# Decay products of a chunked scan: contraction over all 128 rows with a masked left tile

## The chip, the cores and the metric

One core of a Trainium2 chip. The metric is device time in microseconds (us) for one execution of the whole kernel. TensorE (PE) multiplies, VectorE (DVE), ScalarE (ACT) and GpSimd (POOL) do the elementwise work, and SyncE (SP) issues the DMAs; each engine takes its own instructions in order and waits on semaphores for the others.

## What is computed

One step of a hybrid decoder layer over 1,024 prompt tokens and 32 sample tokens: a spatial-gating MLP, a Mamba-2 scan and a memory attention read the same normalised input, and one output projection joins them. The change lies in the scan. It works in chunks of 128 tokens, and inside a chunk each of 8 heads needs a 128 x 128 matrix of decays:

```
acum   = jnp.cumsum(dt * a, axis=2)                       # running sums of the chunk
diff   = acum[:, :, :, None] - acum[:, :, None, :]
decay  = jnp.exp(jnp.where(causal, diff, -jnp.inf))
y_diag = jnp.einsum('bclgn,bcsgn,bclsgk,bcsgkp->...', cm, bm, decay, x * dt)
```

## The kernel before, in words

Nearly all of the time goes to projections. Every float32 operand is split into a part H and a remainder L, and a projection is a triple of matmuls for each of 8 row blocks (`gemm3`, L290 H x H, L291 L x H or H x L, L292 the third), here of 128 x 128 by 352 columns. Other work runs beside them: after each row block `hook()` adds a pace to a counter, and each time it passes 1 it runs the next step of a generator. So the order of the instructions on every engine is fixed when the program is built: a step's instructions stand between two triples on PE.

While the q, gg and part of the mg projections run, that generator is `scan()` (L825 on). It has 16 chunks, 2 groups of heads by 8 chunks of tokens, and in the loop over chunk i it prepares chunk i + 1:

- `sC(i)`: the chunk's C is split into CH (ACT, L107) and CL (DVE, L110).
- `sA(i + 1)`, L755 to L775: four transposes and a C B product on PE, then on DVE `xdt` (L772), `cbm` (L773) and `BL` (L110), on POOL `xsD` (L775).
- one step later `sE(i + 1, 0)`, and one step after that `sE(i + 1, 1)`: the decay products of four heads each, L808. `sE(i, 0)` is followed on ACT by Relu and Exp (L813, L815), `sE(i, 1)` by a min on DVE (L812) and an Exp on ACT (L816). `sM` (L820) multiplies the result `MT` by `cbm` on DVE.
- then the products with the state and into it (`mm3`, L797 to L799, contraction over 128 rows, 512 columns), `hT` times the chunk's decay on POOL (L877), 16 small products L882, and the elementwise tail (L888, L889, L903, L718, L906, L732 on DVE).

A decay product makes diff for four heads by 512 columns at once: the left tile holds 8 + 8 rows of negated running sums (H and L) and two rows of ones, the right tile the ones that pick a head and the running sums as rows. That is 18 rows for a chunk. The tiles `Lt` and `Rt` (128 rows) hold four chunks, chunk i on the 18 rows from q = 32 (i % 4) on, and the product takes these rows of both. The raw rows arrive in `Lraw` and `Rraw` by DMA: `chunk_rows` (L611 to L619) issues 16 DMAs for four chunks on SP (L617, L618), and `lr_copy`, once in four chunks, casts both to float32r on DVE (L750, L751) and calls `chunk_rows` for the next four.

The stream of weights runs beside that: at the end of some gemms (`w_tick`) a unit of 128 x 1024 is split, `wh` on ACT (L107), `wl` on DVE (L110), and SP's DMA of a later unit (L169) waits for that `wl`.

Of the kernel before, what the change touches and what calls it, by code (L numbers as in the profile page):

```python
# [58 lines left out]
def hybrid_step(ctx, tc, x_prompt, x_sample, mem_prompt, state_ssm, state_conv, cache_mem_k,  # L59
# [25 lines left out]
    # every float32 operand of the large products is split exactly into a float32r part (H) and  # L85
    # a float32r remainder (L); products are H*H + H*L + L*H, accumulated in float32
# [17 lines left out]
    def split(raw, H, L, heng, leng):  # L104
        """H = float32r(raw), L = raw - H"""
        if heng is ACT:
            ACT.activation(out=H, in_=raw, func=AF.Copy)  # L107
        else:
            heng.tensor_copy(out=H, in_=raw)
        leng.tensor_tensor(out=L, in0=raw, in1=rb(H), op=ALU.subtract)  # L110

# [114 lines left out]
    # 1 where the token belongs to the batch: 0 <= p - 4 b <= 3  # L226
# [17 lines left out]
    class RowNorm:  # L244
        """rows xt [T, 1024] -> dH + dL [128, 8, T] = (rmsnorm(xt) * g)^T"""

        bufs = 2
# [25 lines left out]
    # work that runs beside the large products: stepped between their parts  # L273
# [12 lines left out]
    def gemm3(ps, lhs, rhs, k0, kn, first, last, mid=None):  # L286
        """ps += sum over k of lhs(k)^T rhs(k) in three float32r products"""
        for k in range(k0, k0 + kn):
            (lH, lL), (rH, rL) = lhs(k), rhs(k)
            PE.matmul(out=ps, lhsT=lH, rhs=rH, start=(first and k == k0), stop=False)  # L290
            PE.matmul(out=ps, lhsT=lH, rhs=rL, start=False, stop=False)  # L291
            PE.matmul(out=ps, lhsT=lL, rhs=rH, start=False, stop=(last and k == k0 + kn - 1))  # L292
            if mid is not None and k == 3:
                mid()
            hook()
# [10 lines left out]
    def gemmA(w, mH, mL, t0, n):  # L306
        """weights stationary: [128 channels, n tokens]"""
        ps = mm()
        gemm3(ps[:, :n], lambda k: (w[0][:, k, :], w[1][:, k, :]),
              lambda k: (mH[:, k, t0:t0 + n], mL[:, k, t0:t0 + n]), 0, KD, True, True)  # L310
        w_tick()
        return ps

    def gemmS(wp, n, dst):
        """the 32 sample tokens stationary, H and L side by side: [dst = 32 tokens, n channels]; the weights
        are released"""
        ps = mm()
        for k in range(KD):
            wH, wL = wp[k // 4][0][:, k % 4, :], wp[k // 4][1][:, k % 4, :]
            if k > 0:  # L320
                PE.matmul(out=ps[:32, :n], lhsT=xS[:, k, 0:32], rhs=wL, start=False, stop=False)
            PE.matmul(out=ps[:64, :n], lhsT=xS[:, k, :], rhs=wH, start=(k == 0), stop=(k == KD - 1))
            if k == 0:
                PE.matmul(out=ps[:32, :n], lhsT=xS[:, k, 0:32], rhs=wL, start=False, stop=False)
            if k == 3:
                w_half()
            hook()
        w_done(1)
        ACT.activation(out=dst, in_=ps[:32, :n], func=AF.Copy)
        DVE.tensor_tensor(out=dst, in0=dst, in1=ps[32:64, :n], op=ALU.add)  # L330
        w_tick()

    def gemmB(mH, mL, t0, T, wp, n, last=False):
        """tokens stationary: [T tokens, n channels]; after the last tile the weights are released"""
        ps = mm()
        gemm3(ps[:T, :n], lambda k: (mH[:, k, t0:t0 + T], mL[:, k, t0:t0 + T]),
              lambda k: (wp[k // 4][0][:, k % 4, :], wp[k // 4][1][:, k % 4, :]), 0, KD, True, True,
              w_half if last else None)
        if last:
            w_done(1)  # L340
        w_tick()
        return ps

    # =====================================================================
    # Phase B: Mamba-2
    # =====================================================================
# [22 lines left out]
    Lt = bp.tile([128, 128], F32R, name="Lt")  # L369

# [24 lines left out]
    # the activation table is loaded while the first rows arrive  # L395
# [15 lines left out]
    def setup_side():  # L411
# [5 lines left out]
        # conv state, transposed  # L417
# [7 lines left out]
        # rows of the decay products: rows 0-7 and 8-15 pick a head (1 on its columns), 16-17 hold  # L425
        # the running sums (H, L) of the chunk
        POOL.memset(Lraw, 1.0)
        POOL.memset(Rraw, 1.0)
        POOL.affine_select(out=Rraw[0:8], in_=Rraw[0:8], pattern=[[1, 8], [0, 128]], compare_op=ALU.is_equal,
# [49 lines left out]
    # parameter vectors, one 128-vector per row, then transposed  # L479
# [22 lines left out]
    def x_side(t):  # L502
        # beside the products of tile t: transposes of tile t + 1, norm of tile t + 2
        if t + 5 < NTILE:
            x_load(t + 5)
        if t + 1 < NTILE:
            rn[t + 1].s2(0)
            yield
            rn.pop(t + 1).s2(1)
            if t + 1 == NTILE - 1:  # L510
                ACT.activation(out=xS[:, :, 0:32], in_=rb(xH[:, :, NP:NT]), func=AF.Copy)
                DVE.tensor_copy(out=xS[:, :, 32:64], in_=rb(xL[:, :, NP:NT]))
            yield
        if t + 3 < NTILE:
            x_s1a(t + 3)
            rn[t + 3].s1b()
# [18 lines left out]
    def dt_chain(pool):  # L535
# [10 lines left out]
        # log1p(e) = ln(u) * e / (u - 1), or e where u == 1  # L546
# [9 lines left out]
        # dta = -exp(a_log) * dt  # L556
# [46 lines left out]
        chunk_rows(0)  # L603
        for _ in range(4):
            yield
        DVE.tensor_copy(out=Lt, in_=Lraw)
        DVE.tensor_copy(out=Rt, in_=Rraw)
        chunk_rows(4)

    def chunk_rows(i0):  # L610
        """rows of chunk i % 8 of group i // 8, four of them"""  # L611
        for i in range(i0, i0 + 4):
# [3 lines left out]
            for e in range(2):  # L616
                SP.dma_start(out=Lraw[q + 8 * e:q + 8 * e + 8, :], in_=neg_d[e, r0:r0 + 8, :])  # L617
# [98 lines left out]
    def gate_norm(pool, y, sz, T):  # L716
        """y = y * sz; returns the scale to unit mean square; y, sz [T, 512]; sz is overwritten"""
# [29 lines left out]
    def lr_copy(i):  # L747
        """decay rows of chunks i .. i + 3"""
        if i < 16:
            DVE.tensor_copy(out=Lt, in_=Lraw)  # L750
            DVE.tensor_copy(out=Rt, in_=Rraw)  # L751
            if i + 4 < 16:
                chunk_rows(i + 4)

    def sA(i):  # L755
# [8 lines left out]
        s_.cbm = cp.tile([128, 128], F32, tag="cbm", name="cbm", bufs=1)  # L764
        ps = sd()
# [22 lines left out]
    def sC(i):  # L788
        """the chunk's C, for the product with the state"""
# [11 lines left out]
    def sE(i, j):  # L801
        """masked decays of four heads (transposed): exp(min(diff, 0))"""
        q = 32 * (i % 4)
        s_ = S[i]
        if j == 0:
            s_.MT = cp.tile([128, 8, 128], F32, tag="MT", name="MT", bufs=2)
        ps = sd()
        PE.matmul(out=ps, lhsT=Lt[q:q + 18, :],  # L808
                  rhs=Rt[q:q + 18, 4 * j:4 * j + 4, :].rearrange("p h l -> p (h l)"), start=True, stop=True)
# [19 lines left out]
    def scan():  # L829
# [14 lines left out]
        for i in range(16):  # L844
# [35 lines left out]
            for h in range(8):  # L880
# [3 lines left out]
                if h == 3:  # L884
                    if (i + 2) % 4 == 0:
                        lr_copy(i + 2)
# [53 lines left out]
    def sample_scan(sp2):  # L940
# [39 lines left out]
        # H, L, H of B against H, H, L of x: one pass over 96 rows  # L980
# [111 lines left out]
    def softmax_rows(pool, ps, n):  # L1092
        """ps [128, n, 256] scores -> P [128, n, 256]"""
# [133 lines left out]
    # =====================================================================  # L1227
    # Phase A: spatial-gating MLP
    # =====================================================================
# [90 lines left out]
    def mix(h):  # L1320
        """mixes head h; the result takes the place of v: vt[:, c, h] = [channels, tokens of chunk c]"""
# [52 lines left out]
    TB = [(0, 384), (384, 384), (768, 288)]  # L1374

    def outproj(H, L, first, at=None):
        units = [(ct, b) for ct in range(8) for b in range(3)]
        if first:
            # the last tokens are split last
            units[2:5] = units[3:5] + units[2:3]  # L1380
# [34 lines left out]
    def splitA(c, leng=DVE):  # L1415
        """all heads of token tile c"""
# [53 lines left out]
    # =====================================================================  # L1470
    # Phase C: memory cross-attention
    # =====================================================================
# [168 lines left out]
    def y_load(i):  # L1641
        """summed output of the other branches: the block's tokens of one channel tile"""
# [23 lines left out]
    # the output weights stay: the first ones in the slots of the stream  # L1666
# [20 lines left out]
    def rows_part(b, ct):  # L1687
        """transposes of one channel tile back to token rows, plus the residual"""
# [15 lines left out]
        if ct in SQE:  # L1704
# [12 lines left out]
            # the gain, once the squares are taken  # L1717
# [91 lines left out]
```

## Time and profile before

| | us |
|---|---|
| median of 3 runs | 1352.23 (1350.95 to 1352.24) |
| span of the profiled execution | 1351.7 |
| PE busy | 1320.8 (98%) |
| DVE busy | 590.4 (44%) |
| ACT busy | 496.5 (37%) |
| POOL busy | 210.4 (16%) |

For the profiled execution only its span is given, no separate device time; the median lies 0.5 us above the span. In rows of a timeline the first two numbers are the start in us from the start of the span and the duration in us, then engine, line, operation, output tile <- input tiles, shapes, and the count; square brackets give the idle time before it and what ended it. Matmuls overlap in these rows, so what one costs is read from the start of one to the start of the next. In a row of a group, "xN | busy, mean" is the count, the busy us and the mean ns of one. PEclk is the granted TensorE clock as a share of 2.4 GHz. The scan's decay products stand between 269 and 462 us of the span.

### The profile page before, as it was taken

What the parts mean: (1) busy time and instruction counts of PE and PEld (TensorE: products, weight loads), DVE (VectorE), ACT (ScalarE), POOL (GpSimd) and SP (SyncE); (2) the same over time, 40 slices, a digit from 0 to 9 for tenths busy, and PEclk for the clock granted to TensorE, in tenths of its full rate; (3) what the DMA queues carried; (4) which work ended last, traced back from release to release, by engine and by line L of the source; (5) the groups of instructions that cost most, each with busy time, mean ns of one, the idle gap of its engine ahead of it and who ended that gap; (6) DMA issues with size and microseconds to landing.
All of it is one profiled execution on the core that took longest, in us unless ns stands there. A gap on an engine that the chain in (4) does not pass through costs nothing. (4 is left out here: it accounts for less than half of the span.)

```text
span 1351.7 us, 22582 instructions
## 1 busy us (share of the span) xinstructions
PE 1320.8 (98%) x9231; PEld 1236.4 (91%) x9231; DVE 590.4 (44%) x943; ACT 496.5 (37%) x962; POOL 210.4 (16%) x274
## 2 busy tenths in 40 slices
PE   8999999999999999999999999999999889999996
PEld 7999999988888898888779999998999889999996
DVE  6212545566767632422112245345312646654543
ACT  6323444464545432222211124344313633322322
POOL 4200000043434424200000010002000600000122
PEclk9999999999999999999999999999999999999999
DMA  6223111122222245475551114221423565436432
GB/s 223 78 77 99 44 48 48 47 88 76 78 72 88 82 118 165 149 226 179 181 181 45 32 32 127 68 68 44 144 93 128 177 178 182 151 117 193 139 121 95
DMA packets 171595, 151.44 MB, mean 112 GB/s; under 512 B 13781, under 2 KB 155049, under 8 KB 171493
## 3 DMA queue, kind: packets, MB, share of 16 engines
q1 hardware_dynamic: 171492, 150.01, 36.1%
q8 instruction: 72, 1.18, 0.4%
q14 instruction: 31, 0.25, 0.1%
HBM read 111.97 MB, written 37.79 MB: 111 GB/s over the span
## 5 line engine op out<-in xcount | busy, mean ns | idle before, releaser
L290 PE MATMUL ps_mm<-xH,wh 128*128 128x352 f32 x1056 | 359.9, 341 | 0.0
L292 PE MATMUL ps_mm<-xH,wl 128*128 128x352 f32 x1056 | 339.6, 322 | 0.0
L291 PE MATMUL ps_mm<-xL,wh 128*128 128x352 f32 x1056 | 339.2, 321 | 0.0
L290 PEld LDWEIGHTS ps_mm<-xH,wh 128*128 128x128 f32 x1056 | 198.3, 188 | 25.3 <-issue 21.0
L291 PEld LDWEIGHTS ps_mm<-xL,wh 128*128 128x128 f32 x1056 | 199.0, 188 | 0.7
L292 PEld LDWEIGHTS ps_mm<-xH,wl 128*128 128x128 f32 x1056 | 198.4, 188 | 0.0
L110 DVE TENSOR_TENSOR wl<-wr,wh 128x1024 fp32r<-128x1024 f32 (+2 forms) x106 | 121.8, 1161 | 175.2 <-ACT wh L107 174.8
L290 PE MATMUL ps_mm<-wh,xH 128*128 128x256 f32 (+1 forms) x512 | 148.0, 289 | 0.0
L291 PE MATMUL ps_mm<-wl,xH 128*128 128x256 f32 (+1 forms) x512 | 146.4, 286 | 0.1
L292 PE MATMUL ps_mm<-wh,xL 128*128 128x256 f32 (+1 forms) x512 | 145.6, 284 | 0.3 <-DVE xL L110 0.3
L107 ACT ACTIVATE wh<-wr 128x1024 fp32r<-128x1024 f32 (+3 forms) x113 | 101.7, 915 | 36.2 <-PE ps_mm L291 14.2
L292 PEld LDWEIGHTS ps_mm<-wh,xL 128*128 128x128 f32 x512 | 98.1, 192 | 0.6 <-DVE xL L110 0.5
L290 PEld LDWEIGHTS ps_mm<-wh,xH 128*128 128x128 f32 x512 | 97.8, 191 | 0.4
L291 PEld LDWEIGHTS ps_mm<-wl,xH 128*128 128x128 f32 x512 | 97.7, 191 | 0.4 <-POOL wl L110 0.4
L701 ACT ACTIVATE gt<-ps_mm 128x352 f32<-128x352 f32 x72 | 33.0, 458 | 98.2 <-PE ps_mm L292 77.1
L290 PE MATMUL ps_mm<-aH,wh 128*128 128x384 f32 (+1 forms) x192 | 62.7, 327 | 1.9 <-ACT gt L1403 1.0
L290 PE MATMUL ps_mm<-bH,wh 128*128 128x384 f32 (+1 forms) x192 | 64.0, 334 | 0.0
L291 PE MATMUL ps_mm<-aL,wh 128*128 128x384 f32 (+1 forms) x192 | 63.0, 328 | 0.3
L292 PE MATMUL ps_mm<-bH,wl 128*128 128x384 f32 (+1 forms) x192 | 62.4, 325 | 0.2 <-DVE wl L110 0.2
L291 PE MATMUL ps_mm<-bL,wh 128*128 128x384 f32 (+1 forms) x192 | 62.5, 326 | 0.0
L292 PE MATMUL ps_mm<-aH,wl 128*128 128x384 f32 (+1 forms) x192 | 61.9, 323 | 0.0
L1720 POOL TENSOR_TENSOR xres<-xres,gfin 128x1536 f32<-128x1536 f32 (+3 forms) x6 | 14.4, 2392 | 231.6 <-ACT junk L1714 231.6
(385 smaller groups left out, 2472.8 us busy)
## 6 DMA issues: line engine op xcount, KB each, us to landing
wr<-in_w_in_dram SPq DMA_DIRECT2D x60, 512.0 KB
wr<-in_w_out_dram SPq DMA_DIRECT2D x24, 512.0 KB
kv<-in_cache_mem_k_dram SPq DMA_DIRECT2D x16, 512.0 KB
kv<-in_cache_mem_v_dram SPq DMA_DIRECT2D x16, 512.0 KB
y_d<-gt SPq DMA_DIRECT2D x32, 192.0 KB
q_d<-gt SPq DMA_DIRECT2D x24, 176.0 KB
gg_d<-gt SPq DMA_DIRECT2D x24, 176.0 KB
mg_d<-gt SPq DMA_DIRECT2D x24, 176.0 KB
```

What stands on the lines that cost most here:

```text
L107: ACT.activation(out=H, in_=raw, func=AF.Copy)
L110: leng.tensor_tensor(out=L, in0=raw, in1=rb(H), op=ALU.subtract)
L290: PE.matmul(out=ps, lhsT=lH, rhs=rH, start=(first and k == k0), stop=False)
L291: PE.matmul(out=ps, lhsT=lH, rhs=rL, start=False, stop=False)
L292: PE.matmul(out=ps, lhsT=lL, rhs=rH, start=False, stop=(last and k == k0 + kn - 1))
L701: ACT.activation(out=t[:, :BLK], in_=ps[:, :BLK], func=func)
L1720: eng.tensor_tensor(out=t[:, 0:nf, c0:c0 + w], in0=t[:, 0:nf, c0:c0 + w], in1=gc.unsqueeze(1).to_broadcast([128, nf, w]), op=ALU.mult)
```

## The change

`Lt` is no longer a tile for four chunks. A mask `qmask` [128, 4] holds 1 on rows 32q to 32q + 17 of column q, 0 elsewhere. `sA(i)` begins with a new instruction on DVE, which multiplies all of `Lraw` by the mask's column of the chunk and writes a float32r tile `Lt` of the chunk's own; right behind it the two DMAs for the L rows of chunk i + 4 are issued. The product takes all 128 rows of `Lt` and of `Rt`. The R rows keep their cast and their DMAs once in four chunks.

```diff
+        POOL.memset(qmask, 0.0)
+        for q in range(4):
+            POOL.memset(qmask[32 * q:32 * q + 18, q:q + 1], 1.0)
...
-        chunk_rows(0)
+        r_rows(0)
+        for i in range(4):
+            l_rows(i)
...
-        DVE.tensor_copy(out=Lt, in_=Lraw)
         DVE.tensor_copy(out=Rt, in_=Rraw)
-        chunk_rows(4)
+        r_rows(4)
...
+    def l_rows(i):
+        if i < 16:
+            g, c = divmod(i, 8)
+            q = 32 * (i % 4)
+            r0 = c * 16 + g * 8
+            for e in range(2):
+                SP.dma_start(out=Lraw[q + 8 * e:q + 8 * e + 8, :], in_=neg_d[e, r0:r0 + 8, :])
...
-    def lr_copy(i):
+    def r_copy(i):
         if i < 16:
-            DVE.tensor_copy(out=Lt, in_=Lraw)
             DVE.tensor_copy(out=Rt, in_=Rraw)
             if i + 4 < 16:
-                chunk_rows(i + 4)
+                r_rows(i + 4)
...
     def sA(i):
...
+        s_.Lt = cp.tile([128, 128], F32R, tag="Lt", name="Lt", bufs=1)
+        DVE.tensor_scalar(out=s_.Lt, in0=Lraw, scalar1=qmask[:, i % 4:i % 4 + 1], scalar2=None, op0=ALU.mult)
+        l_rows(i + 4)
         ps = sd()
...
     def sE(i, j):
-        q = 32 * (i % 4)
         s_ = S[i]
...
-        PE.matmul(out=ps, lhsT=Lt[q:q + 18, :],
-                  rhs=Rt[q:q + 18, 4 * j:4 * j + 4, :].rearrange("p h l -> p (h l)"), start=True, stop=True)
+        PE.matmul(out=ps, lhsT=s_.Lt, rhs=Rt[:, 4 * j:4 * j + 4, :].rearrange("p h l -> p (h l)"), start=True, stop=True)
```

On DVE, in the stretch where the scan passes from chunk 7 to chunk 8 (a unit of weights is split there, and C of chunk 7), before:

```order
L718 TENSOR_TENSOR xsD<-xsD,sz 128x512
L906 TENSOR_TENSOR hL<-hT,hH 128x512
L732 TENSOR_TENSOR xsT<-ps_sd,vecs 128x4x128
L110 TENSOR_TENSOR wl<-wr,wh 128x1024
L110 TENSOR_TENSOR CL<-bcT,CH 128x128
L772 TENSOR_TENSOR xdt<-ps_sd,dt_all 128x512
L773 TENSOR_TENSOR cbm<-ps_sd,triu 128x128
L110 TENSOR_TENSOR BL<-ps_sd,BH 128x128
```

The same place after the change:

```order
L730 TENSOR_TENSOR xsD<-xsD,sz 128x512
L919 TENSOR_TENSOR hL<-hT,hH 128x512
L744 TENSOR_TENSOR xsT<-ps_sd,vecs 128x4x128
L110 TENSOR_TENSOR wl<-wr,wh 128x1024
L110 TENSOR_TENSOR CL<-bcT,CH 128x128
L778 TENSOR_SCALAR Lt<-Lraw,qmask 128x128
L787 TENSOR_TENSOR xdt<-ps_sd,dt_all 128x512
L788 TENSOR_TENSOR cbm<-ps_sd,triu 128x128
L110 TENSOR_TENSOR BL<-ps_sd,BH 128x128
```

The new instruction that makes the chunk's `Lt` stands behind the split of C (and of the weights, where there is one) and ahead of `xdt`.

On PE, around the first decay product of a chunk, with the semaphores that the product waits for, before:

```order
L292 MATMUL ps_mm<-xH,wl 128x352
L808 MATMUL ps_sd<-Rt,Lt 128x512 [waits DVE_49]
L290 MATMUL ps_mm<-xH,wh 128x352
L291 MATMUL ps_mm<-xL,wh 128x352
L292 MATMUL ps_mm<-xH,wl 128x352
```

The same place after the change:

```order
L292 MATMUL ps_mm<-xH,wl 128x352
L822 MATMUL ps_sd<-Rt,Lt 128x512 [waits DVE_49,PE_49]
L290 MATMUL ps_mm<-xH,wh 128x352
L291 MATMUL ps_mm<-xL,wh 128x352
L292 MATMUL ps_mm<-xH,wl 128x352
```

No instruction moved on PE. The product waited for DVE before as well, for the last DVE instruction that read its PSUM bank; now the instruction waited for is the one that makes `Lt`, one step ahead. PE_49 is PE's own count.

## Rows read from the trace of the kernel before

**Rows 1.** The page: busy time of PE over the whole span, and the granted TensorE clock in 40 slices of it, in tenths (9 is 90% or more).

```profile
PE 1320.8 (98%) x9231; PEld 1236.4 (91%) x9231; DVE 590.4 (44%) x943; ACT 496.5 (37%) x962; POOL 210.4 (16%) x274
...
PEclk9999999999999999999999999999999999999999
```

**Rows 2.** Timeline of PE around one decay product, 300.2 to 301.5 us.

```profile
300.38 0.32 PE L292 MATMUL ps_mm<-xH,wl 128*128 128x352 f32 x1
300.63 0.50 PE L808 MATMUL ps_sd<-Rt,Lt 18*128 18x512 f32 x1
301.06 0.43 PE L290 MATMUL ps_mm<-xH,wh 128*128 128x352 f32 x1
301.33 0.32 PE L291 MATMUL ps_mm<-xL,wh 128*128 128x352 f32 x1
```

**Rows 3.** The line L808 by itself: count, least, median and greatest duration in ns, first and last start in us.

```profile
L808 PE MATMUL ps_sd<-Rt,Lt x32: 489/496/500, 269.1 to 461.3; 18*128 18x512 f32 x32
```

**Rows 4.** Timeline of PE where products over 128 rows with 512 columns pass back into the triples, 304.6 to 305.4 us.

```profile
304.64 0.39 PE L798 MATMUL ps_sd<-xdL,BH 128*128 128x512 f32 x1
304.87 0.39 PE L799 MATMUL ps_sd<-xdH,BL 128*128 128x512 f32 x1
305.10 0.32 PE L290 MATMUL ps_mm<-xH,wh 128*128 128x352 f32 x1
305.26 0.32 PE L291 MATMUL ps_mm<-xL,wh 128*128 128x352 f32 x1
```

**Rows 5.** Groups of instructions on DVE: the cast of `Lt` that goes, and two of the same kind as the new instruction, with a source in SBUF (L1744) and in PSUM (L812).

```profile
L750 DVE CAST Lt<-Lraw 128x128 fp32r<-128x128 f32 x3 | 0.7, 218 | 0.0
...
L1744 DVE TENSOR_SCALAR xres<-xres,rs 128x512 f32<-128x512 f32 x8 | 3.5, 482 | 1.4 <-POOL rs L1732 1.4
...
L812 DVE TENSOR_SCALAR MT<-ps_sd 128x512 f32<-128x512 f32 x16 | 11.0, 687 | 9.2 <-PE ps_sd L808 9.2
```

**Rows 6.** Timeline of PE: the projection's matmul right ahead of the first decay product of chunks 0, 1, 7, 8, 13 and 14.

```profile
268.82 0.32 PE L292 MATMUL ps_mm<-xH,wl 128*128 128x352 f32 x1
...
274.21 0.32 PE L292 MATMUL ps_mm<-xH,wl 128*128 128x352 f32 x1
...
353.57 0.32 PE L292 MATMUL ps_mm<-xH,wl 128*128 128x352 f32 x1
...
366.72 0.32 PE L292 MATMUL ps_mm<-xH,wl 128*128 128x352 f32 x1
...
433.17 0.32 PE L292 MATMUL ps_mm<-xH,wl 128*128 128x352 f32 x1
...
446.34 0.32 PE L292 MATMUL ps_mm<-xH,wl 128*128 128x352 f32 x1
```

**Rows 7.** Timeline of DVE: what stands right ahead of the place of the new instruction at chunks 0, 1, 3, 7, 8 (two rows), 13 and 14.

```profile
268.64 0.83 DVE L662 SCALAR_TENSOR_TENSOR bcT<-raw,vecs,bcT 128x32 f32<-128x32 f32 x3
...
276.13 1.29 DVE L820 TENSOR_TENSOR MT<-MT,cbm 128x512 f32<-128x512 f32 x2 [0.96 <-ACT MT L816]
...
298.92 0.29 DVE L110 TENSOR_TENSOR CL<-bcT,CH 128x128 fp32r<-128x128 f32 x1 [0.31 <-ACT CH L107]
...
352.45 1.21 DVE L110 TENSOR_TENSOR CL<-bcT,CH 128x128 fp32r<-128x128 f32 x1 [0.65 <-ACT CH L107]
...
365.99 1.74 DVE L110 TENSOR_TENSOR wl<-wr,wh 128x1024 fp32r<-128x1024 f32 x1 [0.92 <-ACT wh L107]
367.65 1.13 DVE L110 TENSOR_TENSOR CL<-bcT,CH 128x128 fp32r<-128x128 f32 x1
...
432.03 1.22 DVE L110 TENSOR_TENSOR CL<-bcT,CH 128x128 fp32r<-128x128 f32 x1 [0.66 <-ACT CH L107]
...
447.29 1.13 DVE L110 TENSOR_TENSOR CL<-bcT,CH 128x128 fp32r<-128x128 f32 x1
```

**Rows 8.** Timeline of POOL: what runs there when DVE comes to the place of the new instruction, at chunks 1, 7, 8, 13 and 14.

```profile
277.21 1.35 POOL L110 TENSOR_TENSOR xdL<-xde,xdH 128x512 fp32r<-128x512 f32 x1 [3.95 <-ACT xdH L107]
...
353.46 1.10 POOL L775 TENSOR_TENSOR xsD<-xsD,dsk_b 128x512 f32<-128x512 f32 x1
...
368.60 1.09 POOL L877 TENSOR_TENSOR hT<-hT,dec 128x512 f32<-128x512 f32 x1
...
433.06 1.09 POOL L775 TENSOR_TENSOR xsD<-xsD,dsk_b 128x512 f32<-128x512 f32 x1
...
448.23 1.09 POOL L877 TENSOR_TENSOR hT<-hT,dec 128x512 f32<-128x512 f32 x1
```

**Rows 9.** Waits of PE over the whole span: line waited at, releaser, us in total, times, longest.

```profile
PE ps_sd L1561 <- DVE qL L110: 3.5, 1, 3.5
...
PE ps_mm L292 <- DVE woL L110: 2.1, 1, 2.1
```

**Rows 10.** Busy time by stretch: window, its length, then busy us (instructions) of PE, PEld, DVE, ACT and POOL, the granted TensorE clock, DMA share and GB/s. The first two follow the 3.5 us wait of the rows before, the third the 2.1 us wait.

```profile
1106.00:1108.00 2.00, 2.00 (x11) 2.00 (x10) 0.02 (x1) 1.89 (x4) 0.00 (x0) 0.52 0.92 286
1108.00:1110.00 2.00, 2.00 (x9) 2.00 (x8) 1.43 (x5) 1.05 (x3) 0.00 (x0) 0.63 0.30 100
...
1270.00:1272.00 2.00, 2.00 (x7) 1.92 (x8) 2.00 (x4) 0.00 (x0) 0.00 (x0) 0.50 0.00 0
```

**Rows 11.** Waits of SP between 268 and 480 us: its DMA of a weight unit, us in total, times, longest.

```profile
SPq L169 <- DVE wl L110: 68.2, 10, 9.7
```

**Rows 12.** Weight loads of PE (PEld) in the scan's stretch, 268 to 476 us.

```profile
L291 PEld LDWEIGHTS ps_mm<-xL,wh 128*128 128x128 f32 x257 | 48.6, 189 | 0.7
```

More of the change, by code (lines that the diff above doesn't have):

```diff
@@ L368, in hybrid_step @@
     Rt = bp.tile([128, 8, 128], F32R, name="Rt")
-    Lt = bp.tile([128, 128], F32R, name="Lt")
+    qmask = bp.tile([128, 4], F32, name="qmask")
     sc_ctx = ExitStack()
@@ L602, in dt_chain, with r_rows @@
         yield
-        chunk_rows(0)
+        r_rows(0)
+        for i in range(4):
+            l_rows(i)
         for _ in range(4):
             yield
-        DVE.tensor_copy(out=Lt, in_=Lraw)
         DVE.tensor_copy(out=Rt, in_=Rraw)
-        chunk_rows(4)
-    def chunk_rows(i0):
+        r_rows(4)
[6 more added lines that the diff above has]
+                SP.dma_start(out=Lraw[q + 8 * e:q + 8 * e + 8, :], in_=neg_d[e, r0:r0 + 8, :])
+    def r_rows(i0):
         for i in range(i0, i0 + 4):
@@ L616, in chunk_rows @@
             for e in range(2):
-                SP.dma_start(out=Lraw[q + 8 * e:q + 8 * e + 8, :], in_=neg_d[e, r0:r0 + 8, :])
                 SP.dma_start(out=Rraw[q + 16 + e:q + 17 + e].rearrange("p h l -> p (h l)"),
@@ L885, in scan @@
                     if (i + 2) % 4 == 0:
-                        lr_copy(i + 2)
+                        r_copy(i + 2)
                     if c > 0:
```

## The prediction

> **What bounds the kernel now.** I read the page first: PE is busy 98% of a span of 1351.7 us, at a granted clock of 9 tenths or more in all 40 slices [rows 1]. So time is won or lost only on PE, as matmul time or as new idle time, and DVE (44%), ACT and POOL matter only where PE waits for them. Next came the timeline of PE around one decay product, read from start to start. The L292 ahead of it begins at 300.38, the product at 300.63, the L290 behind it at 301.06 and the next L291 at 301.33 [rows 2]. So 0.95 us pass from that L292 to that L291. All 32 products look like this (489 to 500 ns each) [rows 3]. Then I read the same timeline where products over 128 rows with the same 512 columns run: they follow each other every 0.23 us, and the first triple member behind them is also back after 0.23; members of a triple follow each other every 0.16 [rows 4]. Last I read DVE and POOL at the place where the new instruction will stand.
>
> **The gain: the product itself.** With 128 rows the product should sit in the stream like those of L798 and L799. From L292 to L291 that makes 0.16 (L292 to the product), 0.23 (the product) and 0.16 (L290 to L291), together 0.55 in place of 0.95 [rows 2, 4]. A product gains 0.40 us and 32 of them **12.8 us**. The columns stay 512, so the gain is not in the arithmetic but in the empty time on both sides: 0.25 in place of 0.16 ahead, 0.43 in place of 0.23 under the product, and 0.27 in place of 0.16 behind the L290. The Trainium skill names the cause that fits (TensorEngine Tiling (Array Packing), section Tiling Modes, Key Properties): a change of tiling mode, here to 32 rows and back, drains TensorE; no number stands there, and the traces so far agree as far as 0.40 us a product goes.
>
> **The price: a wait for DVE.** Before, both operands lay ready for chunks. Now `sE(i, 0)` needs `Lt(i)`, which DVE makes one step ahead of it, and DVE takes its work in order, so whatever stands before `Lt(i)` there comes first. For each chunk I compare when PE wants to start, which is the start of the L292 ahead plus 0.16, with when `Lt` could be done: the end of what DVE does before it, plus the new instruction. That instruction is not in the trace; the nearest row is the cast of the same tile that it replaces, 0.22 [rows 5], and I take 0.2.
>
> - Chunk 0: wanted at 268.82 + 0.16 = 268.98; DVE is in the convolution until 268.64 + 0.83 = 269.47; ready at 269.67, late by 0.7 [rows 6, 7].
> - Chunk 1: wanted at 274.37; DVE multiplies both halves of `MT` of chunk 0 until 277.42; ready at 277.62, late by 3.25 [rows 6, 7]. Before, nothing on PE needed that in this step.
> - Chunks 7, 10, 12 and 13 (first and last shown): the split CL ends at 353.66 and 433.25, `Lt` is ready at 353.86 and 433.45, wanted at 353.73 and 433.33; late by 0.1 each [rows 6, 7].
> - Chunks 8, 11 and 14 (first and last shown): a unit of weights is split ahead of CL (365.99 for 1.74), so CL ends at 368.78 and 448.42; `Lt` at 368.98 and 448.62, wanted at 366.88 and 446.50; late by 2.1 each [rows 6, 7].
> - Chunks 2 to 6, 9 and 15: in time. At chunk 3 CL ends at 299.21 and the product was wanted at 300.54 [rows 2, 7].
>
> The lateness adds up to 0.7 + 3.25 + 4 x 0.1 + 3 x 2.1 = 10.7 us. In each of these 9 chunks the weight load (`Lt` is the stationary side) can't run ahead under other matmuls; it takes 0.19 [rows 12], so up to 9 x 0.19 = 1.7 more: **12.4 us**, about the whole gain.
>
> **Does the new instruction wait for POOL?** CL alone took 0.29 (chunk 3) and 1.13 to 1.22 where POOL was at work [rows 7, 8]: an operation on DVE with two sources in SBUF doesn't go on while POOL has its turn. The new one has one source (and a column of scalars). No row shows such an operation beside POOL, so I bound it: 0.2, or 0.2 after the end of the POOL operation under way. POOL does run at just these places [rows 8]: to 278.56 at chunk 1, to 354.56 and 434.15 at chunks 7 and 13, to 369.69 and 449.32 at chunks 8 and 14. With that wait the lateness is 4.4, about 1.0 each, and 3.0 each: 0.7 + 4.4 + 4 x 1.0 + 3 x 3.0 = 18.1, with the loads **19.8 us**. I take this end: CL is the nearest row, and one-source work of this kind runs faster from SBUF than from PSUM at the same size (482 against 687 ns) [rows 5], so from SBUF it seems to be served by more than one path, as CL is. The Trainium skill has a rule that speaks against the change here (SBUF — State Buffer, section Who interferes with whom): `tensor_scalar` can enter a mode that holds the port pair shared with GpSimd, and whichever engine began first blocks the other for its whole instruction. By it the lateness is the 19.8, without it the 12.4.
>
> **What an idle PE does to the clock.** PE's wait of 3.5 us at L1561 was followed by two stretches of 2 us at a granted clock of 0.52 and 0.63, near the 1.2 GHz level [rows 9, 10]; that costs 2 x 0.48 + 2 x 0.37 = 1.7 us. Behind the wait of 2.1 us the clock was at 0.50 [rows 9, 10]. The stalls at chunks 1, 8, 11 and 14 are 2.1 us and longer, so up to 4 x 1.7 = **6.8 us**; the bounds are 0 and 6.8, and I take 6.8, because 3.0 to 4.4 us are nearest to the 3.5.
>
> **What costs nothing.** DVE loses four casts and gains 16 operations of 0.2, at most about 1.3 each with POOL's turn: 20 us on an engine with more than half of the span free [rows 1]; behind `Lt`, `xdt` and `cbm` come later by that, at most 1.5 us of backlog, which I keep for the range. The memsets of the mask stand ahead of the scan on POOL, 16% busy [rows 1]. The DMAs are as many as before, spread out: two behind each `Lt`, which are needed a chunk later, some 12 us. SP then waits for `Lt` in its queue, ahead of spills, `sz` and weight loads, but it already stands waiting for `wl` for up to 9.7 us [rows 11], so it is early. The next chunk's `Lt` waits for those two DMAs, which have most of a chunk.
>
> **Sum.** -12.8 + 19.8 + 6.8 = +13.8; 1351.7 + 13.8 = **1365.5 us**. The median of the runs is 1352.23, 0.5 above the span, so I leave it at that.
>
> **Rivals.**
> - *One of the two costs is absent.* No wait for POOL, but the clock: -12.8 + 12.4 + 6.8 = +6.4. POOL's turn, but no fall: -12.8 + 19.8 = +7.0. About 1358.5. For it: neither cost is shown for this instruction or in this stretch.
> - *Neither.* -12.8 + 12.4 = -0.4: 1351, no change. Against it: it needs both bounds at their kind end.
> - *Faster: DVE is early enough.* The deciding point is whether `Lt` is done before L292 + 0.16. At chunks 8, 11 and 14 DVE stands idle 0.92 ahead of `wl`, for ACT's `wh` [rows 7]; if these operations come earlier relative to PE, or PE's order around the step leaves 2 us more, the lateness of three chunks goes and with it the falls. Left are chunk 0 (0.7), chunk 1 (3.25) and 1.7 of clock: -12.8 + 0.7 + 3.25 + 1.7 + 0.4 = -6.8, 1345. Against it: PE waits for nothing there now, so nothing pulls DVE forward.
> - *The product doesn't get shorter.* If 0.95 stays, because the empty time belongs to the step between two kinds of products and not to the 18 rows, the gain is 0 and the time +26.6 at the full price, 1378. Against it: L290 behind L799 comes after 0.23 [rows 4].
>
> **How the numbers follow.** Both costs 0.40; one of them 0.28; neither 0.15; faster 0.13; no shorter product 0.04. The range leaves out the last and most of the faster case: low 1350.5 (neither, less 0.5), high 1369.5 (the forecast, with 1.5 of backlog twice and 1 of clock). What a measurement can tell from no change is about 0.2%, 2.7 us. Faster by more: 0.13 (the faster case); within: 0.15 (neither); slower: 0.72 (the other three).
>
> **What would show it.** In the profile after, 0.55 from the L292 ahead of a product to the L291 behind it, where PE doesn't wait; waits of PE at the product's line (L822) for DVE's `Lt` in chunks 0, 1, 8, 11 and 14, of 2 us and more in the last four; durations of the new instruction near 0.2 or above 1 (the wait for POOL); granted clock under 1 behind those waits. I am wrong if PE shows no wait for `Lt`, or if the 0.95 stays.

## The result, and the profile after

The changed kernel is slower: a median of 1369.36 us (1364.93 to 1374.23, four runs) against 1352.24 (four runs), ratio 1.0127 with a 95% interval of 1.0094 to 1.016. The profiled execution has a span of 1364.2 us, 12.5 more than before (forecast: 13.8 more); it belongs to one of the two shorter runs.

The page of the changed kernel, busy time and granted TensorE clock in tenths over 40 slices, answers to [rows 1]:

```profile
PE 1316.1 (96%) x9231; PEld 1241.8 (91%) x9231; DVE 605.0 (44%) x955; ACT 495.7 (36%) x962; POOL 210.5 (15%) x279
...
PEclk9999999989999999999999999999999999999999
```

PE is busy for 4.7 us less, yet the span is longer: PE now stands idle for longer. And in slice 9 (273 to 307 us) the clock is under 9 tenths, which it was nowhere before.

Timeline of PE around a product that waited for nothing (chunk 9), answering to [rows 2]:

```profile
386.17 0.32 PE L292 MATMUL ps_mm<-xH,wl 128*128 128x352 f32 x1
386.33 0.40 PE L822 MATMUL ps_sd<-Rt,Lt 128*128 128x512 f32 x1
386.57 0.32 PE L290 MATMUL ps_mm<-xH,wh 128*128 128x352 f32 x1
386.73 0.32 PE L291 MATMUL ps_mm<-xL,wh 128*128 128x352 f32 x1
```

From the L292 to the L291 it is 0.56 us, where it was 0.95: the gain is there. The first product of chunk 8, on PE, and what DVE and POOL did (answering to [rows 6 to 8]):

```profile
368.97 0.32 PE L292 MATMUL ps_mm<-xH,wl 128*128 128x352 f32 x1
372.17 0.76 PE L822 MATMUL ps_sd<-Rt,Lt 128*128 128x512 f32 x1 [2.87 <-DVE Lt L778]
372.73 0.49 PE L290 MATMUL ps_mm<-xH,wh 128*128 128x352 f32 x1
```

```profile
276.48 1.29 DVE L778 TENSOR_SCALAR Lt<-Lraw,qmask 128x128 fp32r<-128x128 f32 x1
...
368.24 1.74 DVE L110 TENSOR_TENSOR wl<-wr,wh 128x1024 fp32r<-128x1024 f32 x1 [0.92 <-ACT wh L107]
369.91 1.12 DVE L110 TENSOR_TENSOR CL<-bcT,CH 128x128 fp32r<-128x128 f32 x1
370.96 1.06 DVE L778 TENSOR_SCALAR Lt<-Lraw,qmask 128x128 fp32r<-128x128 f32 x1
...
384.00 0.28 DVE L778 TENSOR_SCALAR Lt<-Lraw,qmask 128x128 fp32r<-128x128 f32 x1
```

```profile
276.36 1.33 POOL L110 TENSOR_TENSOR xdL<-xde,xdH 128x512 fp32r<-128x512 f32 x1 [3.95 <-ACT xdH L107]
...
370.85 1.09 POOL L890 TENSOR_TENSOR hT<-hT,dec 128x512 f32<-128x512 f32 x1
```

The product was wanted at 368.97 + 0.16 = 369.13 and began at 372.17, 3.04 late. DVE made `Lt` behind `wl` and CL, and took 1.06 for it while POOL's `hT` ran; at chunk 1 (first row) 1.29 while POOL's `xdL` ran; at chunk 9 (last row), with POOL idle, 0.28. Behind the wait the matmuls themselves take longer (0.76, 0.49): the granted clock fell. Over all chunks, three views follow: the new instruction (count; least, median, greatest duration in ns), PE's waits (total, times, longest), and the 12 us stretches in which the clock is low at the four long waits (length, then busy us and count of PE, PEld, DVE, ACT and POOL, granted clock, DMA share, GB/s):

```profile
L778 DVE TENSOR_SCALAR Lt<-Lraw,qmask x16: 278/1060/1316, 268.7 to 472.2; 128x128 fp32r<-128x128 f32 x16
```

```profile
PE ps_sd L822 <- DVE Lt L778: 16.4, 9, 4.0
...
PE ps_sd L1574 <- DVE qL L110: 2.0, 1, 2.0
```

```profile
276.00:288.00 12.00, 10.08 (x69) 9.22 (x70) 5.64 (x10) 4.13 (x9) 3.33 (x3) 0.72 0.25 79
...
372.00:384.00 12.00, 11.84 (x87) 10.87 (x88) 6.96 (x13) 3.73 (x9) 1.05 (x1) 0.88 0.28 88
...
408.00:420.00 12.00, 9.16 (x49) 8.63 (x48) 8.87 (x13) 6.34 (x13) 4.62 (x5) 0.86 0.29 82
...
456.00:468.00 12.00, 9.15 (x55) 8.19 (x54) 8.52 (x12) 4.33 (x10) 4.00 (x4) 0.86 0.32 96
```

Two of the 16 new instructions took under 0.3 us (chunks 0 and 9). Each of the other 14 ended 0.08 to 0.09 us behind the end of a POOL instruction that had begun before it, as in the rows of chunks 1 and 8 above (277.77 behind 277.69, 372.02 behind 371.94). The scan's other stretches stand at a granted clock of 0.98 or more.

### The profile page after: what moved, and what is told of

Its sections match the earlier page's. It is cut to its first block, busy times and chain, and to the rows that moved or that the text cites. A ratio compares the mean times of both kernels' runs of the same rounds, so it can differ in the third digit from the quotient of the medians.

```text
span 1364.2 us, 22630 instructions
## 1 busy us (share of the span) xinstructions
PE 1316.1 (96%) x9231; PEld 1241.8 (91%) x9231; DVE 605.0 (44%) x955; ACT 495.7 (36%) x962; POOL 210.5 (15%) x279
## 5 line engine op out<-in xcount | busy, mean ns | idle before, releaser
L292 PE MATMUL ps_mm<-xH,wl 128*128 128x352 f32 x1056 | 342.2, 324 | 0.0
L291 PE MATMUL ps_mm<-xL,wh 128*128 128x352 f32 x1056 | 342.0, 324 | 0.0
L291 PEld LDWEIGHTS ps_mm<-xL,wh 128*128 128x128 f32 x1056 | 201.5, 191 | 2.4
L292 PEld LDWEIGHTS ps_mm<-xH,wl 128*128 128x128 f32 x1056 | 200.7, 190 | 0.0
L291 PE MATMUL ps_mm<-wl,xH 128*128 128x256 f32 (+1 forms) x512 | 146.4, 286 | 0.1
L292 PE MATMUL ps_mm<-wh,xL 128*128 128x256 f32 (+1 forms) x512 | 145.5, 284 | 0.0
L292 PEld LDWEIGHTS ps_mm<-wh,xL 128*128 128x128 f32 x512 | 98.1, 192 | 0.1
L291 PEld LDWEIGHTS ps_mm<-wl,xH 128*128 128x128 f32 x512 | 97.6, 191 | 0.4 <-POOL wl L110 0.4
L291 PE MATMUL ps_mm<-aL,wh 128*128 128x384 f32 (+1 forms) x192 | 63.0, 328 | 0.3 <-DVE aL L110 0.2
L291 PE MATMUL ps_mm<-bL,wh 128*128 128x384 f32 (+1 forms) x192 | 62.0, 323 | 0.0
L292 PE MATMUL ps_mm<-bH,wl 128*128 128x384 f32 (+1 forms) x192 | 62.0, 323 | 0.0
L292 PE MATMUL ps_mm<-aH,wl 128*128 128x384 f32 (+1 forms) x192 | 61.9, 323 | 0.0
```

## The experiments

Times are medians. lt_ahead, rows18, lt_ahead_4 and lt_ahead_rest ran beside the kernel before, whose median was 1354.98 us there; the others ran beside it at 1353.86. Each ratio is against that median.

**lt_ahead: the product as changed, its left tile a chunk earlier.**

```diff
+    Lts = [bp.tile([128, 128], F32R, name="Lt%d" % e) for e in range(2)]
+    def lt_make(i):
+        DVE.tensor_scalar(out=Lts[i % 2], in0=Lraw, scalar1=qmask[:, i % 4:i % 4 + 1], scalar2=None, op0=ALU.mult)
+        l_rows(i + 4)
...
     def sA(i):
...
-        s_.Lt = cp.tile([128, 128], F32R, tag="Lt", name="Lt", bufs=1)
-        DVE.tensor_scalar(out=s_.Lt, in0=Lraw, scalar1=qmask[:, i % 4:i % 4 + 1], scalar2=None, op0=ALU.mult)
-        l_rows(i + 4)
+        s_.Lt = Lts[i % 2]
...
+        if 2 <= i + 1 < 16:
+            lt_make(i + 1)
```

Chunks 0 and 1 are made in `dt_chain`; `dta` takes the buffer of `xr`, which is dead by then, to make room for the second tile.

> Each chunk's Lt is made a chunk earlier, behind the last DVE instruction of sA for the chunk before, in one of two buffers (chunks 0 and 1: behind the first cast of Rt, long before the scan). Same products over 128 rows, same instruction on DVE, same DMAs. Theory (the products gain 0.40 us each, all of the loss is PE's wait for Lt and the clock that falls behind it): no wait of PE for Lt, granted clock 1.00 in the scan, and the span of before less 32 x 0.40 = 12.8: 1339, up to 1341 if the instruction delays min and the rest behind it. Rival (the 128-row product is no gain by itself): about 1352, with 0.95 from the L292 ahead to the L291 behind. Rival (the instruction, wherever it stands, takes POOL's or DVE's time that PE needs later): 1345 or more, with new waits of PE in the scan.

Measured: 1342.66 us (1342.3 to 1345.08), ratio 0.9913 [0.9899, 0.9928], 12.3 us less than before; span 1340.6. The product's line (least, median, greatest ns) and the whole stretch of the scan, columns as above:

```profile
L832 PE MATMUL ps_sd<-Rt,Lt x32: 389/391/505, 269.8 to 451.2; 128*128 128x512 f32 x32
```

```profile
264.00:480.00 216.00, 214.72 (x1697) 198.71 (x1696) 155.94 (x251) 111.07 (x229) 81.59 (x97) 1.00 0.28 85
```

From the L292 ahead to the L291 behind, the 32 products take 12.4 us less than in the trace before (0.38 to 0.41 each, 0.22 at one), no product waits for `Lt`, and the clock stays at 1.00 in the scan. Without the wait the product's shape is a gain, and this version beats both kernels. Not all of it arrives: from the L292 ahead of the first product to the L291 behind the last, PE gains 11.2 us. Most of the missing 1.2 us is at one place, the first product into the state (`ps_sd<-xdH,BH`): PE stands idle for 1.11 us ahead of it, where it was 0.27 in the trace before.

**rows18: the wait without the gain.**

```diff
-        PE.matmul(out=ps, lhsT=s_.Lt, rhs=Rt[:, 4 * j:4 * j + 4, :]...
+        q = 32 * (i % 4)
+        PE.matmul(out=ps, lhsT=s_.Lt[q:q + 18], rhs=Rt[q:q + 18, 4 * j:4 * j + 4, :]...
```

> The changed kernel, with the product alone put back to the chunk's 18 rows of Lt and Rt; the masked Lt is made at the same place, so PE waits for it as in the change. Theory: the gain of 32 x 0.40 goes and the waits stay: 1364.2 + 12.8 = 1377, or about 1 less, because behind a stall PE is empty anyway. PE waits for Lt of about 16 us, clock falls at chunks 1, 8, 11 and 14 as in the change. Rival (the product's rows make no difference to the time): 1364.

Measured: 1387.12 us (1380.71 to 1389.15), 32.1 more than before where 25 was expected; span 1386.5. The wait of PE in the scan, and the stretches behind chunk 1's wait, chunk 8's (two neighbouring ones) and chunk 11's:

```profile
PE ps_sd L823 <- DVE Lt L778: 15.8, 9, 3.4
```

```profile
276.00:288.00 12.00, 9.06 (x26) 7.54 (x26) 6.26 (x10) 4.71 (x10) 3.33 (x3) 0.59 0.26 75
372.00:384.00 12.00, 9.13 (x48) 7.77 (x47) 8.55 (x12) 5.78 (x12) 4.61 (x5) 0.86 0.30 81
384.00:396.00 12.00, 12.00 (x90) 10.59 (x88) 4.96 (x9) 2.04 (x6) 3.11 (x4) 0.85 0.05 16
420.00:432.00 12.00, 9.16 (x39) 7.62 (x38) 7.78 (x11) 6.08 (x13) 4.61 (x5) 0.71 0.29 82
```

The waits are those of the change, nine of them. From the L292 ahead of the first product to the L291 behind the last, this trace loses 31.0 us on the trace before, the changed kernel 14.2: 16.8 apart. The products are at most 12.4 of that; behind a wait of about 1 us the two shapes are only 0.2 apart (at chunk 10, 1.66 us from the L292 ahead to the L291 behind in the changed kernel, 1.85 here). The rest, 4.4 us or more, I put down to the clock, which stays low for longer here: over the scan it is granted 0.93 (264 to 498 us), in the changed kernel 0.96 (264 to 480 us). That split is argued, and why the clock stays low for longer with 18-row products wasn't tested.

**lt_ahead_4 and lt_ahead_rest: the two halves of the wait.** `lt_make(i)` is called early for chunks 1, 8, 11 and 14 alone, or for all the others alone; where it isn't called early, it stands at the change's place.

```diff
+    AHEAD = (1, 8, 11, 14)
...
+        if i not in AHEAD:
+            lt_make(i)
...
+        if 2 <= i + 1 < 16 and i + 1 in AHEAD:
+            lt_make(i + 1)
```

> Lt is made a chunk earlier for chunks 1, 8, 11 and 14 alone, the four whose wait was 3.0 to 4.1 us and was followed by a lower clock; the others as in the change. Theory: of the wait 0.97 + 4 x 1.05 + 0.46 + 0.29 = 5.9 us are left, none over 1.3, and the clock stays at 1.00: 1339 + 5.9 = 1345. Rival (the clock fell for another reason than these waits): about 7 us more, 1352, with granted clock under 1 in the scan.

> The complement: Lt is made a chunk earlier for all chunks but 1, 8, 11 and 14. Theory: their waits stay, 4.13 + 3.04 + 3.01 + 3.01 = 13.2 us, and with them the clock's loss of about 7.2: 1339 + 20.4 = 1359. Rival (the clock fell for another reason): 1352, with the clock at 1.00 behind the waits.

Measured: lt_ahead_4 1350.42 us (1348.85 to 1351.4), 7.8 over lt_ahead where 6 was expected. Its waits for `Lt` and the two halves of the scan:

```profile
PE ps_sd L832 <- DVE Lt L373: 4.9, 6, 1.4
```

```profile
264.00:372.00 108.00, 105.12 (x812) 96.09 (x810) 82.86 (x132) 56.82 (x116) 41.06 (x49) 1.00 0.27 82
372.00:480.00 108.00, 104.81 (x842) 96.10 (x840) 78.07 (x121) 52.29 (x109) 40.57 (x48) 1.00 0.26 78
```

Six waits up to 1.4 us, and the clock stays at 1.00 in the scan. lt_ahead_rest measured 1359.34 us, but its ten runs lie between 1354.72 and 1367.79. The profiled one took 1356.25. Its waits follow, then three of the four on PE (chunks 8, 11 and 14), and the stretches around all four:

```profile
PE ps_sd L832 <- DVE Lt L373: 13.1, 4, 4.5
```

```profile
370.21 0.47 PE L832 MATMUL ps_sd<-Rt,Lt 128*128 128x512 f32 x1 [2.88 <-DVE Lt L373]
...
410.59 0.77 PE L832 MATMUL ps_sd<-Rt,Lt 128*128 128x512 f32 x1 [2.87 <-DVE Lt L373]
...
452.57 0.47 PE L832 MATMUL ps_sd<-Rt,Lt 128*128 128x512 f32 x1 [2.86 <-DVE Lt L373]
```

```profile
276.00:288.00 12.00, 9.76 (x61) 8.96 (x63) 6.13 (x11) 4.45 (x10) 3.33 (x3) 0.72 0.27 83
360.00:372.00 12.00, 9.12 (x83) 8.32 (x82) 8.78 (x13) 4.93 (x11) 5.66 (x6) 1.00 0.23 63
372.00:384.00 12.00, 12.00 (x100) 11.06 (x99) 6.13 (x10) 4.25 (x10) 3.03 (x4) 1.00 0.12 40
408.00:420.00 12.00, 9.41 (x69) 8.43 (x70) 8.36 (x15) 3.62 (x7) 3.41 (x3) 0.86 0.33 98
444.00:456.00 12.00, 9.14 (x70) 8.39 (x70) 9.07 (x14) 5.94 (x13) 4.60 (x5) 1.00 0.28 82
```

The same wait was followed twice by the full clock (chunks 8 and 14, 2.88 and 2.86 us: the product takes 0.47, the stretches stand at 1.00) and once by the low one (chunk 11, 2.87 us: 0.77, 0.86). So in the scan the falls belong to the long waits (with the waits of lt_ahead_4, up to 1.4 us, there is none), but not to each of them. In the ten runs the time goes with the clock over the whole execution: the six runs up to 1359.39 us have a mean granted clock of 0.989 to 0.991, the four longer ones 0.984 to 0.987.

**after_again: is that the scatter?** The changed kernel, unedited.

> The changed kernel itself beside the others of this job, since its runs lay at 1365 and at 1373 and lt_ahead_rest's between 1355 and 1368: if the clock's fall behind a wait of some 3 us comes in some executions and not in others, the times scatter by several us here too, and the profile shows waits for Lt of about 19 us again while the slices of low clock differ from the first profile's (all of chunks 1, 8, 11 and 14). If the scatter has another cause, the same four falls show.

Measured: 1370.49 us (1367.27 to 1371.96), ratio 1.0132 [1.0115, 1.0148]; span 1370.2, 6.0 above the first profile's. Stretches as above:

```profile
276.00:288.00 12.00, 8.04 (x43) 7.24 (x43) 7.00 (x12) 6.14 (x12) 3.33 (x3) 0.72 0.27 76
372.00:384.00 12.00, 9.13 (x55) 8.15 (x54) 7.82 (x12) 3.08 (x7) 3.66 (x3) 0.86 0.33 96
...
420.00:432.00 12.00, 12.00 (x92) 11.05 (x90) 8.39 (x13) 4.86 (x11) 3.22 (x5) 0.90 0.14 48
456.00:468.00 12.00, 9.15 (x49) 8.57 (x48) 8.43 (x12) 6.22 (x13) 4.58 (x5) 0.86 0.33 97
```

The clock falls behind all four long waits again, in the same places (the stretches have moved by some us), and PE waits 16.6 us for `Lt`, where the first profile has 16.4. By the expectation that speaks for another cause of the scatter. The traces say where: the scan loses 14.7 us on the trace before, the first profile's 14.2, so only 0.5 of the 6.0 us between the two spans lie in the scan. Of the rest 2.4 lie ahead of it (the first product starts at 269.11 and 271.54) and 3.1 behind it. The four runs here are within 4.7 us, so the spread of the first four, 1364.93 to 1374.23, wasn't seen again; its cause stays open.

**lt_act: another engine at the same place.**

```diff
-        DVE.tensor_scalar(out=s_.Lt, in0=Lraw, scalar1=qmask[:, i % 4:i % 4 + 1], scalar2=None, op0=ALU.mult)
+        ACT.activation(out=s_.Lt, in_=Lraw, func=AF.Copy, scale=qmask[:, i % 4:i % 4 + 1])
```

> The changed kernel, with Lt made on ACT (a copy scaled by the mask's column) at the same place of the program; nothing is moved ahead. If the wait comes from what stands in front of it on DVE and from POOL's turn, ACT has little of both: by the rows of before CH ends at 352.42 and 366.50 at chunks 7 and 8, so Lt is there at 352.7 and 366.8, wanted at 353.73 and 366.88: waits of 0 to 0.3 where the change had 1.05 and 3.04. Chunk 0 stands behind ACT's bcT (to 270.65): 1.9 to 2.1; chunk 1 behind xdH (to 277.1): 3.0 to 3.3. Together 5 to 6 us, one fall of the clock at most: 8 to 10 us under after_again's neighbourhood of 1367 less again the three long waits, in all some 1346 to 1349 where before is 1355. Rival (the place in the program, one step ahead, is too late whoever makes it): waits like the change's, 1365.

Measured: 1346.57 us (1344.29 to 1349.72), ratio 0.9951 [0.9931, 0.9972].

```profile
PE ps_sd L822 <- ACT Lt L778: 4.8, 3, 2.0
```

```profile
264.00:276.00 12.00, 10.02 (x65) 9.31 (x63) 7.53 (x11) 6.10 (x12) 2.67 (x5) 1.00 0.12 37
276.00:288.00 12.00, 10.19 (x85) 9.38 (x86) 7.04 (x12) 6.48 (x15) 3.52 (x4) 1.00 0.32 91
```

Three products are late: chunk 0's by 2.0 us, chunk 1's by 2.1 (expected were 3.0 to 3.3) and chunk 9's by 1.1 (not foreseen). All others are on time. So one step ahead was not too late as such; what stood ahead on DVE, and POOL, made `Lt` late. The first two waits, up to 2.0 us, lie in the stretches shown, and the clock stays at 1.00 there and in the rest of the scan.

**lt_ahead_k114 and lt_ahead_k64: what the 0.40 us are.** As lt_ahead, with 114 or 64 rows of both tiles in the product.

```diff
-        PE.matmul(out=ps, lhsT=s_.Lt, rhs=Rt[:, 4 * j:4 * j + 4, :]...
+        PE.matmul(out=ps, lhsT=s_.Lt[0:114], rhs=Rt[0:114, 4 * j:4 * j + 4, :]...
...
+        q = 64 * (i % 4 // 2)
+        PE.matmul(out=ps, lhsT=s_.Lt[q:q + 64], rhs=Rt[q:q + 64, 4 * j:4 * j + 4, :]...
```

> As lt_ahead, the product over rows 0 to 113 alone of both tiles (the rows behind are zero in Lt). If the empty time of the 18-row product belongs to a switch between sizes of row groups (32 rows and 128), 114 rows are no switch: 0.55 from the L292 ahead to the L291 behind, 1342 to 1343. If any product that doesn't take all 128 rows empties PE: 0.95, about 1355.

> As lt_ahead, the product over the half of 64 rows that holds the chunk's 18 (rows 0 to 63 or 64 to 127 of both tiles). If a switch to row groups of another size costs the 0.40, 64 rows cost it as 18 do: 0.95 and about 1355. If it is the row groups of 32 alone, or the small number of rows: 0.55 to 0.75, 1342 to 1349.

Measured: 1339.9 us with 114 rows (two runs, ratio 0.9909 [0.9889, 0.9928]), 1353.2 with 64 (1349.11 to 1355.75, ratio 0.9995 [0.9979, 1.001]). PE around one product, 114 rows, then 64:

```profile
299.90 0.32 PE L292 MATMUL ps_mm<-xH,wl 128*128 128x352 f32 x1
300.06 0.39 PE L832 MATMUL ps_sd<-Rt,Lt 114*128 114x512 f32 x1
300.29 0.32 PE L290 MATMUL ps_mm<-xH,wh 128*128 128x352 f32 x1
300.45 0.32 PE L291 MATMUL ps_mm<-xL,wh 128*128 128x352 f32 x1
```

```profile
301.19 0.32 PE L292 MATMUL ps_mm<-xH,wl 128*128 128x352 f32 x1
301.45 0.49 PE L833 MATMUL ps_sd<-Rt,Lt 64*128 64x512 f32 x1
301.87 0.43 PE L290 MATMUL ps_mm<-xH,wh 128*128 128x352 f32 x1
302.13 0.32 PE L291 MATMUL ps_mm<-xL,wh 128*128 128x352 f32 x1
```

0.55 us with 114 rows, 0.94 with 64, the same as with 18. So the 0.40 us belong neither to the number of rows nor to whether all 128 are in use: 64 rows cost what 18 do, and 114 cost what 128 do. The Trainium skill has a rule that fits (TensorEngine Tiling (Array Packing), section Tiling Modes): the configurations are of 32, 64 and 128 rows, and a change of mode drains TensorE. These runs agree as far as the groups go, and give a number for there and back: 0.40 us. That it is a drain, no row shows.

## Why the prediction held, step by step

**The gain, -12.8.** Held: the products of lt_ahead's trace take 12.4 us less, and the medians are 12.3 apart. Over the scan 11.2 arrive and in the spans 11.1, as a longer wait elsewhere takes 0.8 back.

**The lateness, 19.8 with the loads.** Held in sum, and by chunk nearly: the first products of the chunks are 19.3 us late in all, against the L292 ahead plus 0.16. By chunk, late by (forecast with the load of 0.19 in brackets): 0 by 0.97 (0.9); 1 by 4.13 (4.6); 7, 10, 12 and 13 by 1.02 to 1.06 (1.2); 8, 11 and 14 by 3.01 to 3.04 (3.2). The nine forecast chunks make 18.3 of it. Those that wait for POOL came 0.16 us or more earlier than forecast, because a product starts 0.23 behind the end of POOL's instruction (371.94 and 372.17 at chunk 8), where the forecast had 0.2 + 0.19. What failed is "chunks 2 to 6, 9 and 15: in time": chunks 2 and 3 were late by 0.46 and 0.29, because there too the new instruction took 1.31 beside POOL. The forecast had POOL's turn only where it had rows for it.

**POOL's turn.** Held: of the two bounds the upper one came, 1.06 to 1.32 against 0.28 alone. That POOL causes it, lt_ahead shows too: there the same instruction meets POOL's at other moments, takes 0.33 to 0.85 us in ten of the 16, and in each of the ten ends 0.08 to 0.09 us behind POOL's. The Trainium skill (SBUF — State Buffer, section Who interferes with whom) states that `tensor_scalar` can enter a mode that holds the port pair shared with GpSimd, and that whichever engine began first blocks the other for its whole instruction. The traces agree with it by these ends.

**The clock, 6.8.** The size held in the profiled execution: from the L292 ahead of the first product to the L291 behind the last, PE falls 14.2 us behind the trace before; -12.4 and +19.3 make 6.9, and 7.3 are left for the lower clock and what is slower right behind a wait. The four low stretches bear that out: they lose (0.28 + 0.12 + 0.14 + 0.14) x 12 = 8.2 us, an estimate, and less than that as PE stood idle for some of it. The step under it, a price of 1.7 for each wait of 2.1 us and more, did not hold: chunk 1's stretch loses up to 3.4 and the others 1.4 to 1.7, in lt_ahead_rest the clock fell behind two of the four waits alone, and in rows18 it stayed low for longer. That the sum came out near 6.8 is partly luck. The forecast gave this term no spread upwards beyond 1 us.

**The sum.** +13.8 forecast, +14.2 in the scan's stretch, +12.5 in the span. Part of what was lost came back behind the scan: the wait of 3.5 us in [rows 9] (L1561, now L1574) is 2.0. The medians moved by 17.1 and 16.6. So the case came for the reasons given, but they account for the 12.5 of the profiled execution; no trace shows where the medians' further 4 to 5 us come from, and between the two traces of the changed kernel the difference lies mostly outside the scan. The first median is 0.14 us below the upper edge of the range, 1369.5, and five of the eight runs lie above it: that it fell inside is luck, and the range was too tight on the upper side.

**The rivals.** "Faster" needed `Lt` done before L292 + 0.16; lt_ahead and, but for three chunks, lt_act show what that is worth, and the change doesn't have it. "The product doesn't get shorter" fell at chunk 9's 0.56. "One cost absent" and "neither" fell: both costs are in the trace.

## What to carry to other kernels

Here a product over 18 or 64 rows, in the midst of products over 128, took 0.40 us more each time than one over 114 or 128; a zero-padded operand takes that away, at no cost in columns. But an operand that is now made for each use must be costed as a deadline: when the engine that makes it gets to it, in its own order and beside what POOL runs then, against when PE would take it. Made a chunk ahead, the same instruction made no product wait.

## What was not expected of the hardware

A wait of PE of about 2.9 us was followed by the low clock in one place (granted 0.86 over 12 us) and not in two others (1.00) of the same execution, at the same length to 0.01 us. Nor does the length alone order them: the kernel before has a low clock behind a wait of 2.1 us (0.50, [rows 9, 10]). The ten runs of lt_ahead_rest spread over 13.1 us; 14 runs of the kernel before beside it over 5.5, and eight of lt_ahead_k64, without such waits, over 6.6. The clock goes with that spread: 0.984 in the longest run and 0.990 in the shortest are 0.006 x 1360 = 8 us, an estimate. Only one of the ten was traced, so whether falls behind these waits make the difference was not shown.
